# Delta rule: triangles laid in the partitions by block, matrix and head, and one store of the inverses per half of the rows in place of four

## The chip, the cores and the metric

The kernel runs on one core of one Trainium2 chip. The metric is the device time of one execution in microseconds (us). Times given as measured are the median of several runs; a profile is one further execution, recorded by the hardware profiler. A core has five engines that run their own instruction streams: TensorE (PE, with its weight loads PEld), VectorE (DVE), ScalarE (ACT), GpSimd (POOL) and SyncE (SP). DMA transfers are issued by SP (queue q1 in the profile), ACT (q10) and POOL (q0) and are moved by 16 DMA engines.

## The reference, cut to what matters

One layer of a bidirectional hybrid encoder on 256 tokens of width 2048. Branch B is a gated delta rule with 16 heads of width 128, forward and backward. The part that matters here is the unit lower triangular solve of each chunk:

```python
    a_mat = jnp.eye(CHUNK, dtype=jnp.float32) + (
        betac[..., :, None] * jnp.einsum('nbhid,nbhjd->nbhij', kc, kc) * decay_strict)
    t_mat = lax.linalg.triangular_solve(
        a_mat, jnp.broadcast_to(jnp.eye(CHUNK, dtype=jnp.float32), a_mat.shape),
        left_side=True, lower=True, unit_diagonal=True)
    u = jnp.einsum('nbhij,nbhje->nbhie', t_mat, betac[..., None] * vc)
    w = jnp.einsum('nbhij,nbhjd->nbhid', t_mat, (betac * jnp.exp(gc))[..., None] * kc)
```

Beside it stand a chunkwise mLSTM branch, the merge of the two branches and a SwiGLU feed-forward part, all with float32 weights that are read once.

## The kernel before

The bulk of the work is matrix products against weights of 1 MB pieces that SP loads. Each piece is split on the chip into a high part by ACT (wh, L157 and L182) and a low part by DVE (wl, L158 and L183), and PE multiplies with both (L161, L163 and L200 to L203). PE runs in its own order, so a wl that is late holds it up.

The delta rule is woven between these products. The kernel uses chunks of 128 tokens, so a head has four matrices: forward and backward for each of two chunks. Of each matrix only the four diagonal blocks of 32x32 are inverted by elimination; the larger blocks follow by small products.

- `gdn_phase1(h)` (L537) makes the four matrices of head h in the tile mi, partitions = row of the matrix. POOL writes the 16 triangles of the head to the DRAM tile inst_d (four DMAs, L604, one for each diagonal block) and reads them back so that each triangle lies in one partition of the tile uu (one DMA, L607). Four heads make a group (GRP = 4), so uu has 64 partitions of 32x32 numbers. Before the change the 16 triangles of a head lie in 16 neighbouring partitions.
- `gdn_invert(g)` (L619) inverts the 64 triangles of group g on DVE, 30 steps of two instructions (L635, L641). After the step i = 16 the rows 16 to 31 are done, after the last step the rows 0 to 15. `store(rows)` (L625) writes such a half to the DRAM tile inv_d: four POOL DMAs, one for each head, each of 16 partitions (L627). A run of DRAM that is written in one piece has 32 numbers, 128 B.
- `gdn_blocks(g)` (L650) reads inv_d into cg with the four diagonal blocks stacked in the partitions: four POOL DMAs (L654) that wait until both halves are stored. DVE transposes the 32x32 blocks (L656) and mixes them into R (L660, L661); ACT copies them into X (L669) and UL (L674).
- `gdn_phase2(g, p)` (L677) does the products for two heads of the group; its first PE instruction is p1 (L689), which needs R.

The order of instructions on an engine is set by a scheduler with a model of durations of its own, except for those inside `order(...)`, which keep the order of the program. Between `invert(g)` and the first use of cg the main program (L857 to L863) puts eight steps of weight products (`fill(8)`), so that PE, ACT and DVE have work while the inverses go to DRAM and back. Times in the text are from the start of the span. Group 0 passes this place at about 284 to 305 us, group 1 at 472 to 490, group 2 at 658 to 682 and group 3 at 857 to 876.

A weight product is named by its job: o0 and o1, mb1, ma2, a2 and b4, b8, b12 are such jobs, and wl_o1_0_2 is the low part of the second half of the first piece of job o1.

Of the kernel before, what the change touches and what calls it, by code (L numbers as in the profile page):

```python
# [9 lines left out]
F32 = mybir.dt.float32  # L10
# [11 lines left out]
NH_B, DK_B = 16, 128  # L22
# [3 lines left out]
GRP = 4  # L26
# [26 lines left out]
def hybrid_block(ctx: ExitStack, tc: tile.TileContext, xr, nfr, crow, pk_d, cst_d, ada2, ada4, win0, winb, wint, wba, wbb, wo, wgu, wd, out, dbg=None):  # L53
    nc = tc.nc
    V, S, G, PE = nc.vector, nc.scalar, nc.gpsimd, nc.tensor
# [29 lines left out]
    def order(ins, yes=True):  # L85

        return tc.keep_in_program_order(ins) if yes else ins
# [168 lines left out]
    mb_d = [tc.dram_tile([P, 2, 512], F32, name=f"mb_d{g}") for g in range(4)]  # L256
    ob_d = [tc.dram_tile([4, P, T], F32, name=f"ob_d{g}") for g in range(4)]
    inst_d = [tc.dram_tile([64, 32, 32], F32, name=f"inst_d{g}") for g in range(NH_B // GRP)]
    inv_d = [tc.dram_tile([32, 4, 16, 32], F32, name=f"inv_d{g}") for g in range(NH_B // GRP)]

    hh, hl = (bigA.tile([P, KB // 2, 2, 2, P], F32R, tag="b16", name=n) for n in ("hh", "hl"))

# [179 lines left out]
    with ExitStack() as s0:  # L442
        w0 = pool(s0, "w0")

        x = w0.tile([P, KB, T], F32, name="x")
        ss = w0.tile([P, 2], F32, name="ssx")
        rows = w0.tile([P, T], F32, name="rows")
# [87 lines left out]
    uus = {}  # L535

    def gdn_phase1(h):  # L537
# [61 lines left out]
        g, hl_ = divmod(h, GRP)  # L599
        if g not in uus:  # L600
            uus[g] = bk.tile([64, 32, 32], F32, tag="uu", bufs=1, name=f"uu{g}")
        inst = inst_d[g][16 * hl_ : 16 * hl_ + 16]
        for b in range(4):
            G.dma_start(  # L604
                inst[4 * b : 4 * b + 4].rearrange("x j i -> j x i"), mi[32 * b : 32 * b + 32, :, 32 * b : 32 * b + 32]
            )
        G.dma_start(uus[g][16 * hl_ : 16 * hl_ + 16], inst)  # L607

        cc = ccs[h % NB]
        for b in range(4):  # L610
# [8 lines left out]
    def gdn_invert(g):  # L619

        uu = uus.pop(g)
        tmp = bk.tile([64, 256], F32, tag="utmp", bufs=1, name=f"utmp{g}")
        inv = inv_d[g].rearrange("j b (x h) i -> h (b x) j i", h=GRP)

        def store(rows):  # L625
            for e in range(GRP):
                G.dma_start(inv[e, :, rows], uu[16 * e : 16 * e + 16, rows])  # L627

        yield
        order(V.memset(uu.rearrange("p j i -> p (j i)")[:, ::33], 1.0))  # L630
        size = 0
        for i in range(30, 0, -1):
            w = 31 - i
            t3 = tmp[:, 0 : i * w].rearrange("p (j c) -> p j c", j=i)
            order(V.tensor_tensor(  # L635
                t3,
                uu[:, 0:i, i : i + 1].broadcast_to([64, i, w]),
                uu[:, i : i + 1, i + 1 :].broadcast_to([64, i, w]),
                ALU.mult,
            ))  # L640
            order(V.tensor_tensor(uu[:, 0:i, i + 1 :], uu[:, 0:i, i + 1 :], t3, ALU.add))  # L641
            if i == 16:
                store(slice(16, 32))
            size += i * w + 125
            if size > 720:
                size = 0
                yield
        store(slice(0, 16))

    def gdn_blocks(g):  # L650

        cg = bk.tile([P, 2, 512], F32, tag="uu", bufs=1, name=f"cg{g}")
        for b in range(4):
            G.dma_start(cg[32 * b : 32 * b + 32, 0], inv_d[g][:, b].rearrange("j x i -> j (x i)"))  # L654
        yield
        order(V.transpose(cg[:, 1], cg[:, 0]))  # L656
        F_, Bt, Ft, B_ = (cg[:, i // 2, (i % 2) * 256 : (i % 2 + 1) * 256].rearrange("p (m c) -> p m c", m=8) for i in range(4))

        def mix(dst, a, ca, b, cb):
            order(V.tensor_scalar(dst, b, cb, None, ALU.mult))  # L660
            order(V.scalar_tensor_tensor(dst, a, ca, dst, ALU.mult, ALU.add))  # L661

        mix(R[:, 0], Ft, even, Bt, odd)
        mix(R[:, 1], B_, even, F_, odd)
        yield
        for i, ab in enumerate(((Ft, Bt), (B_, F_))):
            for b in range(4):
                r = slice(32 * b, 32 * b + 32)
                order(S.activation(X[r, i, :, b % 2], ab[b // 2][r], AF.Copy))  # L669
            yield  # L670
        for i, a in enumerate((F_, B_)):
            for b in range(4):
                r = slice(32 * b, 32 * b + 32)
                order(S.activation(UL[r, i, :, r], a[r], AF.Copy))  # L674
            yield
# [133 lines left out]
    def stream(h0):  # L809
# [21 lines left out]
        while True:  # L831
            fill(1)
            yield True

    heads1 = {h: gdn_phase1(h) for h in range(NH_B)}
    after = (0, 1, 2, 1, 2, 2, 2, 2, 4, 0)
    last = (0, 1, 2, 1, 2, 2, 1, 1, 3, 0)
# [12 lines left out]
    def invert(g):  # L850
        gen = gdn_invert(g)
        next(gen)
        fill(4)
        for _ in gen:
            fill(1)

    invert(0)  # L857
    for g in range(4):
        blocks = gdn_blocks(g)
        next(blocks)  # L860
        fill(8)
        next(blocks)
        fill(1)  # L863
        pairs = [gdn_phase2(g, p) for p in range(2)]
        every[0] = (0, 2, 2, 2)[g]
        for p in range(2):
            pieces = stream(4 * g + 2 * p + 4)
            for n in range(1, 10):
                next(pairs[p], None)
                if p == 0:  # L870
                    next(blocks, None)
                for _ in range(after[n] if g < 3 else last[n]):
                    next(pieces)
            for _ in pairs[p]:
                pass

            if g < 3:
                while 4 * g + 2 * p + 5 not in heads:
                    next(pieces)
        if g < 3:  # L880
            fills.insert(0, z_job(g + 1))
            every[0] = 0
            invert(g + 1)
# [327 lines left out]
    for j in range(FB // 4):  # L1211
# [4 lines left out]
        for e2 in range(2):  # L1216
            px = gps(f"pxf{j}_{e2}")
            for e in range(2):
                f = 2 * e2 + e
                for t in range(2):  # L1220
                    PE.transpose(px[:, e * T + t * P : e * T + (t + 1) * P], sg[:, t, f * P : (f + 1) * P], ident)
            b = 4 * j + 2 * e2
# [143 lines left out]
```

## Time and profile before

| | us |
|---|---|
| median of 3 runs | 2038.97 (2037.25 to 2042.45) |
| the profiled execution | 2036.88 |
| its span, first to last instruction | 2035.0 |
| PE busy | 1956.7 (96%) |
| DVE busy | 1394.1 (69%) |
| ACT busy | 1050.0 (52%) |
| POOL busy | 106.4 (5%) |

In the timeline a row has the start in us, the duration in us, the engine, the line, the operation, what it writes and reads, how often (x) in a row, and in brackets the idle time of the engine before it and what ended that. The rows of a stretch of time give the length, then for each engine the busy time, then the TensorE clock that was granted (1.00 is full speed), the share of the time in which the DMA engines moved data, and GB/s. The rows of DMA queues give packets, MB and the share of the 16 engines' time. An engine is counted as waiting only if it had nothing else that it was allowed to do.

### The profile page before, as it was taken

The numbers are of one execution on the slowest core, as the hardware profiler recorded it, in microseconds if no ns is written. First come the engines' busy times: TensorE is split into PE (matmuls) and PEld (weight loads), VectorE is DVE, ScalarE is ACT, GpSimd is POOL, SyncE is SP. The second block draws the span as 40 slices with busy tenths as digits, with TensorE's granted clock in tenths as the row PEclk, the third lists the DMA queues.
The fourth block names the chain that finished last, engine by engine and source line by source line (L and its number), as shares of the span: only waits on it lengthen the run. The fifth ranks groups of instructions, "written<-read, shape, count | busy, mean of one in ns | idle before, by whom it ended". The sixth has DMA issues, their size and how long they took to land.

```text
span 2035.0 us, 27065 instructions
## 1 busy us (share of the span) xinstructions
PE 1956.7 (96%) x10374; PEld 1706.4 (84%) x10374; DVE 1394.1 (69%) x2059; ACT 1050.0 (52%) x1582; POOL 106.4 (5%) x205
## 2 busy tenths in 40 slices
PE   8999999999999899999899999999999999999997
PEld 6777879988888788988878788778888888888886
DVE  5778777777889588855677679866666665555554
ACT  3147547755775577565444444554444444444443
POOL 0002210010101010100200000000000000000000
PEclk9999999999999899999999999999999999999999
DMA  9986664556766465766987669656767666566563
GB/s 399 420 325 222 178 215 153 190 171 220 241 230 197 178 211 212 243 238 240 360 297 264 212 245 390 256 186 249 252 244 262 235 246 212 204 206 204 199 200 142
DMA packets 78962, 485.64 MB, mean 239 GB/s; under 512 B 10585, under 2 KB 15969, under 8 KB 24433
## 3 DMA queue, kind: packets, MB, share of 16 engines
q1 hardware_dynamic: 63360, 450.95, 61.2%
q0 software_dynamic: 8160, 17.88, 3.8%
q10 hardware_dynamic: 7314, 15.10, 2.0%
q8 instruction: 81, 1.33, 0.3%
q14 instruction: 47, 0.39, 0.1%
HBM read 467.07 MB, written 16.82 MB: 238 GB/s over the span
## 4 chain that ended last, share of the span: by engine, by line
PE 70%; DMA 11%; DVE 9%; ACT 6%; issue 2%; POOL 1%; ACTq 0%; SPq 0%; DVEq 0%; POOLq 0%
PE acc_up L200 4%; PE acc_up L203 4%; PE acc_up L201 4%; PE acc_d L201 4%; PE acc_d L200 4%; PE acc_d L203 4%; PE acc_gt L201 4%; PE acc_gt L200 4%; PE acc_gt L203 4%; PE acc_b L161 3%; DMA ra<-ada 3%; DMA ada<-ada 2%; PE acc_o L203 2%; PE acc_o L200 2%; PE acc_o L201 2%
## 5 line engine op out<-in xcount | busy, mean ns | idle before, releaser
L183 DVE TENSOR_TENSOR wl_d<-raw_d,wh_d 128x1024 fp32r<-128x1024 f32 x88 | 107.5, 1225 | 105.4 <-ACT wh_d L182 103.1
L183 DVE TENSOR_TENSOR wl_up<-raw_up,wh_up 128x1024 fp32r<-128x1024 f32 x88 | 107.6, 1225 | 100.4 <-ACT wh_up L182 100.4
L126 DVE SCALAR_TENSOR_TENSOR ada<-ada,crow 128x2048 f32<-128x2048 f32 x64 | 146.6, 2290 | 24.1 <-DMA ada<-ada 24.0
L182 ACT ACTIVATE wh_d<-raw_d 128x1024 fp32r<-128x1024 f32 x88 | 92.9, 1056 | 124.5 <-PE acc_d L201 114.3
L183 DVE TENSOR_TENSOR wl_gt<-raw_gt,wh_gt 128x1024 fp32r<-128x1024 f32 x88 | 107.7, 1224 | 69.9 <-ACT wh_gt L182 68.4
L182 ACT ACTIVATE wh_up<-raw_up 128x1024 fp32r<-128x1024 f32 x88 | 92.9, 1057 | 120.9 <-PE acc_up L201 71.6
L161 PE MATMUL acc_b<-hh,wh_b 128*128 128x256 f32 x576 | 142.0, 288 | 9.6 <-ACT wh_b L157 8.0
L182 ACT ACTIVATE wh_gt<-raw_gt 128x1024 fp32r<-128x1024 f32 x88 | 92.9, 1055 | 108.9 <-PE acc_gt L201 61.3
L161 PE MATMUL acc_b<-hl,wh_b 128*128 128x256 f32 x576 | 139.6, 284 | 0.0
L201 PE MATMUL acc_gt<-wh_gt,hfl 128*128 128x512 f32 x352 | 136.9, 389 | 0.0
L200 PE MATMUL acc_gt<-wh_gt,hfh 128*128 128x512 f32 x352 | 135.6, 385 | 0.0
L200 PE MATMUL acc_up<-wh_up,hfh 128*128 128x512 f32 x352 | 133.4, 379 | 0.0
L201 PE MATMUL acc_up<-wh_up,hfl 128*128 128x512 f32 x352 | 133.4, 379 | 0.0
L200 PE MATMUL acc_d<-wh_d,ffh 128*128 128x512 f32 x344 | 130.8, 380 | 0.0
L201 PE MATMUL acc_d<-wh_d,ffl 128*128 128x512 f32 x344 | 130.5, 379 | 0.0
L161 PEld LDWEIGHTS acc_b<-hh,wh_b 128*128 128x128 f32 x576 | 114.6, 199 | 10.2 <-ACT wh_b L157 8.5
L511 PE MATMUL first<-x,raw 128*128 128x256 f32 x512 | 114.5, 382 | 6.6 <-ACT x L504 6.6
L511 PEld LDWEIGHTS first<-x,raw 128*128 128x128 f32 x512 | 96.0, 190 | 25.1 <-ACT x L504 12.6
L161 PEld LDWEIGHTS acc_b<-hl,wh_b 128*128 128x128 f32 x576 | 114.8, 199 | 0.0
L300 DVE SCALAR_TENSOR_TENSOR cv<-pad,pk,cv 128x256 f32<-128x256 f32 x192 | 90.8, 481 | 20.2 <-ACT cv L298 18.2
L158 DVE TENSOR_TENSOR wl_b<-raw_b,wh_b 128x1024 fp32r<-128x1024 f32 x72 | 86.9, 1220 | 23.7 <-ACT wh_b L157 20.6
L182 ACT ACTIVATE wh_o<-raw_o 128x1024 fp32r<-128x1024 f32 x64 | 67.4, 1056 | 60.1 <-PE acc_o L201 27.2
(369 smaller groups left out, 5016.4 us busy)
## 6 DMA issues: line engine op xcount, KB each, us to landing
ada<-ada SPq DMA_DIRECT2D x64, 1024.0 KB, 5.2
raw_gt<-wgu SPq DMA_DIRECT2D x44, 1024.0 KB, 5.0
raw_up<-wgu SPq DMA_DIRECT2D x44, 1024.0 KB, 4.9
raw_d<-wd SPq DMA_DIRECT2D x44, 1024.0 KB, 4.9
raw_b<-winb SPq DMA_DIRECT2D x36, 1024.0 KB, 5.1
ra<-ada SPq DMA_DIRECT2D x32, 1025.0 KB, 15.7
raw<-win SPq DMA_DIRECT2D x16, 1024.0 KB, 14.5
raw_z<-wint SPq DMA_DIRECT2D x16, 1024.0 KB, 5.1
```

Source lines behind the costliest of these rows:

```text
L126: V.scalar_tensor_tensor(raw, raw, 1.0, row_c[:, :D], ALU.mult, ALU.mult, accum_out=mod[:, c0 + b : c0 + b + 1])
L158: V.tensor_tensor(wl, raw[:, k0 : k0 + 8], wh.bitcast(F32), ALU.subtract)
L161: PE.matmul(o, wh[:, k], both(x, k0 + k).rearrange("p a b -> p b a"), start=k0 + k + i == 0, stop=False)
L182: order(S.activation(wh, raws[u][:, k0 : k0 + 2], AF.Copy), early)
L183: order(V.tensor_tensor(wl, raws[u][:, k0 : k0 + 2], wh.bitcast(F32), ALU.subtract), early)
L200: order(PE.matmul(ps[t], tok(xh, kk, t), turns(wh[:, k]), start=kk == 0, stop=False), early and steps > 1)
L201: PE.matmul(ps[t], tok(xl, kk, t), turns(wh[:, k]), start=False, stop=False)
L203: PE.matmul(ps[t], tok(xh, kk, t), turns(wl[:, k]), start=False, stop=kk == last)
L300: V.scalar_tensor_tensor(cv, pd[:, i : i + T], w[i], cv, ALU.mult, ALU.add)
L511: PE.matmul(first[o], raw[:, o], x[:, b], start=b == 0 and o % 2 == 0, stop=b == KB - 1 and o % 2 == 1)
```

## The change

The partition of a triangle in uu is no longer 16 x head + 4 x block + matrix but 16 x block + 4 x matrix + head (head within the group). The load of a head's triangles therefore goes to every fourth partition. The partitions of uu then lie in the order in which inv_d holds the triangles, so that `store(rows)` is one DMA of 64 partitions in place of four of 16. The bytes of inv_d, the four loads of cg and all computation are as they were.

```diff
-    inv_d = [tc.dram_tile([32, 4, 16, 32], F32, name=f"inv_d{g}") for g in range(NH_B // GRP)]
+    inv_d = [tc.dram_tile([32, 64, 32], F32, name=f"inv_d{g}") for g in range(NH_B // GRP)]
...
-        G.dma_start(uus[g][16 * hl_ : 16 * hl_ + 16], inst)
+        G.dma_start(uus[g][hl_::GRP], inst)
...
-        inv = inv_d[g].rearrange("j b (x h) i -> h (b x) j i", h=GRP)
...
         def store(rows):
-            for e in range(GRP):
-                G.dma_start(inv[e, :, rows], uu[16 * e : 16 * e + 16, rows])
+            G.dma_start(inv_d[g][rows].rearrange("j p i -> p j i"), uu[:, rows])
...
-            G.dma_start(cg[32 * b : 32 * b + 32, 0], inv_d[g][:, b].rearrange("j x i -> j (x i)"))
+            G.dma_start(cg[32 * b : 32 * b + 32, 0], inv_d[g][:, 16 * b : 16 * b + 16].rearrange("j m i -> j (m i)"))
```

The scheduler also moves instructions of the weight products around the place where cg is waited for. The order of PE stays as it was. On DVE, group 1, before the change (cg1 is the tile of the inverses, R and wl as above):

```order
L183 TENSOR_TENSOR wl_o1_0_0_4026<-raw_o1_0_4023,wh_o1_0_0_4025 128x1024
L183 TENSOR_TENSOR wl_o1_0_2_4047<-raw_o1_0_4023,wh_o1_0_2_4046 128x1024
L656 STREAM_TRANSPOSE cg1_3894<-cg1_3894 128x512
L660 TENSOR_SCALAR R_1108<-cg1_3894,cst_75 128x256
L158 TENSOR_TENSOR wl_b8_0_0_4077<-raw_b8_0_4074,wh_b8_0_0_4076 128x1024
L661 SCALAR_TENSOR_TENSOR R_1108<-cg1_3894,cst_75,R_1108 128x256
L660 TENSOR_SCALAR R_1108<-cg1_3894,cst_75 128x256
L661 SCALAR_TENSOR_TENSOR R_1108<-cg1_3894,cst_75,R_1108 128x256
```

The same place on DVE after the change:

```order
L183 TENSOR_TENSOR wl_o1_0_0_4014<-raw_o1_0_4011,wh_o1_0_0_4013 128x1024
L654 STREAM_TRANSPOSE cg1_3882<-cg1_3882 128x512
L658 TENSOR_SCALAR R_1108<-cg1_3882,cst_75 128x256
L659 SCALAR_TENSOR_TENSOR R_1108<-cg1_3882,cst_75,R_1108 128x256
L658 TENSOR_SCALAR R_1108<-cg1_3882,cst_75 128x256
L183 TENSOR_TENSOR wl_o1_0_2_4035<-raw_o1_0_4011,wh_o1_0_2_4034 128x1024
L659 SCALAR_TENSOR_TENSOR R_1108<-cg1_3882,cst_75,R_1108 128x256
L158 TENSOR_TENSOR wl_b8_0_0_4065<-raw_b8_0_4062,wh_b8_0_0_4064 128x1024
```

The last wl that PE needs ahead of p1, wl_o1_0_2, stood ahead of the transposition of cg1 and now stands three instructions behind it; wl_b8_0_0 moves two places back. On DVE, group 3, before the change:

```order
L158 TENSOR_TENSOR wl_a2_3_0_8067<-raw_a2_3_8064,wh_a2_3_0_8066 128x1024
L158 TENSOR_TENSOR wl_a2_3_8_8100<-raw_a2_3_8064,wh_a2_3_8_8099 128x1024
L656 STREAM_TRANSPOSE cg3_7852<-cg3_7852 128x512
L660 TENSOR_SCALAR R_1108<-cg3_7852,cst_75 128x256
L661 SCALAR_TENSOR_TENSOR R_1108<-cg3_7852,cst_75,R_1108 128x256
L660 TENSOR_SCALAR R_1108<-cg3_7852,cst_75 128x256
L183 TENSOR_TENSOR wl_ma2_0_0_8146<-raw_ma2_0_8143,wh_ma2_0_0_8145 128x1024
L661 SCALAR_TENSOR_TENSOR R_1108<-cg3_7852,cst_75,R_1108 128x256
```

The same place on DVE after the change:

```order
L158 TENSOR_TENSOR wl_a2_3_0_8043<-raw_a2_3_8040,wh_a2_3_0_8042 128x1024
L654 STREAM_TRANSPOSE cg3_7828<-cg3_7828 128x512
L658 TENSOR_SCALAR R_1108<-cg3_7828,cst_75 128x256
L659 SCALAR_TENSOR_TENSOR R_1108<-cg3_7828,cst_75,R_1108 128x256
L658 TENSOR_SCALAR R_1108<-cg3_7828,cst_75 128x256
L659 SCALAR_TENSOR_TENSOR R_1108<-cg3_7828,cst_75,R_1108 128x256
L158 TENSOR_TENSOR wl_a2_3_8_8076<-raw_a2_3_8040,wh_a2_3_8_8075 128x1024
L183 TENSOR_TENSOR wl_ma2_0_0_8122<-raw_ma2_0_8119,wh_ma2_0_0_8121 128x1024
```

Here wl_a2_3_8, the last low part that PE needs ahead of p1, moves from ahead of the transposition to behind the second R. In group 0 wl_o0_2_0, which stood behind the first instruction on R, stands behind the third; group 2 keeps its order.

On ACT, group 1, the order before (X is what ACT copies from cg1, ev_mb1 empties a PSUM buffer that PE wants again for job b8):

```order
L182 ACTIVATE wh_o1_0_2_4046<-raw_o1_0_4023 128x1024
L157 ACTIVATE wh_b8_0_0_4076<-raw_b8_0_4074 128x1024
L313 ACTIVATE ev_mb1_4017<-acc_mb1_0_3870 128x512
L313 ACTIVATE ev_mb1_4017<-acc_mb1_1_3871 128x512
L669 ACTIVATE X_1109<-cg1_3894 32x8x32
L314 DMA mb_d1_111<-ev_mb1_4017 128x1024
```

The same place on ACT after the change:

```order
L182 ACTIVATE wh_o1_0_2_4034<-raw_o1_0_4011 128x1024
L667 ACTIVATE X_1109<-cg1_3882 32x8x32 x4
L157 ACTIVATE wh_b8_0_0_4064<-raw_b8_0_4062 128x1024
L313 ACTIVATE ev_mb1_4005<-acc_mb1_0_3861 128x512
L313 ACTIVATE ev_mb1_4005<-acc_mb1_1_3862 128x512
L314 DMA mb_d1_111<-ev_mb1_4005 128x1024
```

The four copies into X now stand ahead of wh_b8_0_0 and of ev_mb1.

## Prediction

> **What bounds the kernel now.** I read the page first: the span and the busy shares.
>
> ```profile
> span 2035.0 us, 27065 instructions
> PE 1956.7 (96%) x10374; PEld 1706.4 (84%) x10374; DVE 1394.1 (69%) x2059; ACT 1050.0 (52%) x1582; POOL 106.4 (5%) x205
> ```
>
> PE is nearly always busy, so this change can only pay through the few places where PE stops. Next I asked who waits for the stores (the view of the tile inv_d) and what size they have (the list of DMA issues).
>
> ```profile
> L627 POOL DMA_DIRECT2D inv_d<-uu x32: 562/562/593, 266.5 to 858.3; - x32
>   DVE cg L656: 28.4, 4
>   POOL cg L654: 22.0, 4
> inv_d<-uu POOLq DMA_DIRECT2D x32, 32.0 KB, 3.4
> ```
>
> POOL takes 562 ns to issue one store of 32 KB. It waits 22.0 us in four groups for the stores before it may issue the loads of cg, and DVE waits 28.4 us for these loads. Whether PE pays is seen in the timeline. Group 0:
>
> ```profile
> 284.24 2.23 POOL L627 DMA_DIRECT2D inv_d<-uu  x4 [15.45 <-DVE uu L641]
> 291.24 1.99 POOL L654 DMA_DIRECT2D cg<-inv_d  x4 [4.77 <-DMA inv_d<-uu]
> 299.95 0.71 DVE L656 STREAM_TRANSPOSE cg<-cg 128x512 f32<-128x512 f32 x1 [8.62 <-DMA cg<-inv_d]
> 300.81 1.22 DVE L183 TENSOR_TENSOR wl_o<-raw_o,wh_o 128x1024 fp32r<-128x1024 f32 x1
> 302.08 1.54 PE L203 MATMUL acc_o<-wl_o,hh 128*128 128x512 f32 x4 [3.50 <-DVE wl_o L183]
> ```
>
> So store, wait, load, wait, transposition, wl lie in one chain, and PE stands 3.50 us at its end, until 302.08. The eight steps of filling are too short by that. The stretches around the stops add a second price, the granted clock (the number before the last two):
>
> ```profile
> 298.50:302.00 3.50, 0.08 (x1) 0.00 (x0) 2.05 (x4) 1.21 (x3) 0.00 (x0) 1.00 0.02 6
> 302.00:309.00 7.00, 6.92 (x31) 6.68 (x32) 5.27 (x8) 3.62 (x6) 0.00 (x0) 0.55 0.28 81
> 485.60:488.20 2.60, 0.05 (x1) 0.00 (x0) 2.51 (x5) 1.69 (x5) 0.00 (x0) 1.00 0.37 150
> 678.50:682.00 3.50, 3.44 (x18) 3.44 (x19) 2.36 (x4) 0.49 (x2) 0.00 (x0) 0.56 0.63 192
> ```
>
> After the stop of 3.50 us PE runs 7.0 us at 0.55, which loses 7.0 x 0.45 = 3.15 us; after group 2's stops it loses 3.5 x 0.44 = 1.5 us. After the stop of group 1 (the third row) the clock stayed at 1.00.
>
> Groups 1, 2 and 3, from the timeline:
>
> ```profile
> 472.18 2.22 POOL L627 DMA_DIRECT2D inv_d<-uu  x4 [16.47 <-DVE uu L641]
> 479.04 1.99 POOL L654 DMA_DIRECT2D cg<-inv_d  x4 [4.64 <-DMA inv_d<-uu]
> 484.62 1.03 PE L203 MATMUL acc_o<-wl_o,hh 128*128 128x512 f32 x4
> 485.69 0.71 DVE L656 STREAM_TRANSPOSE cg<-cg 128x512 f32<-128x512 f32 x1 [6.32 <-DMA cg<-inv_d]
> 488.22 1.08 PE L689 MATMUL p<-R,cc 128*128 128x32 f32 x8 [2.57 <-DVE R L661]
> ```
>
> ```profile
> 657.87 2.22 POOL L627 DMA_DIRECT2D inv_d<-uu  x4 [13.10 <-DVE uu L641]
> 665.33 1.99 POOL L654 DMA_DIRECT2D cg<-inv_d  x4 [5.23 <-DMA inv_d<-uu]
> 672.11 0.71 DVE L656 STREAM_TRANSPOSE cg<-cg 128x512 f32<-128x512 f32 x1 [6.48 <-DMA cg<-inv_d]
> 675.03 1.13 PE L203 MATMUL acc_mb<-wl_mb,hh 128*128 128x512 f32 x4 [1.40 <-DVE wl_mb L183]
> 678.56 0.58 PE L161 MATMUL acc_b<-hh,wh_b 128*128 128x256 f32 x1 [1.59 <-ACT ev_ma L313]
> ```
>
> ```profile
> 856.63 2.22 POOL L627 DMA_DIRECT2D inv_d<-uu  x4 [16.49 <-DVE uu L641]
> 866.20 2.00 POOL L654 DMA_DIRECT2D cg<-inv_d  x4 [7.35 <-DMA inv_d<-uu]
> 870.72 1.06 PE L163 MATMUL acc_a<-hh,wl_a 128*128 128x256 f32 x8
> 872.18 0.71 DVE L656 STREAM_TRANSPOSE cg<-cg 128x512 f32<-128x512 f32 x1 [6.99 <-DMA cg<-inv_d]
> 873.79 1.05 PE L689 MATMUL p<-R,cc 128*128 128x32 f32 x8 [2.02 <-DVE R L661]
> ```
>
> All that hangs on these transfers is 3.50 + 2.57 + 1.40 + 1.59 + 2.02 = 11.1 us of stops and 4.7 us of slow clock, 15.8 us together. More than that the change cannot give.
>
> **What the store costs now, and will cost.** The four stores of group 0 were issued from 284.24 to 286.47. The DMA queues of the stretches 284.2 to 287.0 (first row), 287.7 to 289.4 (second) and 289.4 to 290.2 (third) tell when they ran:
>
> ```profile
> q0 software_dynamic: 49, 0.07, 18.1%
> ...
> q1 hardware_dynamic: 87, 0.71, 98.9%
> ...
> q0 software_dynamic: 64, 0.07, 23.2%
> ```
>
> Two stores (2 x 32 KB = 0.07 MB) ran before 287.0. Then a weight load on q1 held the engines at 98.9%, and in this stretch the answer has no row for q0 at all. The other two stores, though issued by 286.47, ran after 289.4, and POOL went on at 291.24. Groups 1 and 2 show the same 6.86 and 7.46 us from the first issue to the loads (479.04 - 472.18, 665.33 - 657.87), group 3 9.57 us. The Trainium skill ("DMA: Bandwidth & Descriptors", Queues, rings and completion order) says that each engine takes turns between its queue rows packet by packet; the trace does not bear that out here, since no packet of q0 moved for 1.7 us.
>
> *One issue in place of four* saves three of 562 ns, 1.7 us, if the issue of 64 partitions costs the same. It writes four times as many pieces of 128 B as one old store. From below: 0.56 us. From above: four times that, 2.25 us, no saving. The widest POOL issue in the trace has 128 x 4 pieces of 1 KB:
>
> ```profile
> 968.31 1.57 POOL L895 DMA_DIRECT2D o<-ob_d  x2 [100.11 <-ACT wh_a L157]
> ```
>
> 0.79 us each for twice the pieces of an old store. I take 0.8 us, so 1.4 us saved.
>
> *One place in the queue in place of four* is the larger part. All packets of the one store stand in the queue from its issue on, so they should run where the first two stores ran, ahead of the weight load. The second old store's last completions fell before 287.7 and POOL needed 291.24 - 290.2 = 1.0 us after the last packets of the others, so the loads of cg would be issued at about 288.7, 2.5 us earlier. They meet the same bursts of weights, so DVE's start moves by more or by less. Call the shift of DVE's transposition S. Bounds: 0 (the store finishes no earlier than four do) and about 5 us (store and load each escape one burst of some 2.5 us). I take S = 3, near the 2.5.
>
> **The sum.** The order of DVE changed, and that must be set against S. The pitch of its instructions after a transposition, from group 3:
>
> ```profile
> 873.56 0.35 DVE L660 TENSOR_SCALAR R<-cg,cst 128x256 f32<-128x256 f32 x1
> 873.82 1.22 DVE L183 TENSOR_TENSOR wl_ma<-raw_ma,wh_ma 128x1024 fp32r<-128x1024 f32 x1
> 874.96 0.48 DVE L661 SCALAR_TENSOR_TENSOR R<-cg,cst,R 128x256 f32<-128x256 f32 x1
> ```
>
> A wl behind three instructions on R starts 873.82 - 872.18 = 1.64 us after the transposition starts and ends 2.86 us after; behind four of them, some 0.4 us later, 3.25.
>
> - Group 0: PE went on 302.08 - 299.95 = 2.13 us after the transposition; now 2.86, 0.73 later. With S = 3 PE gains 2.27 of its 3.50; a stop of 1.2 us should keep the clock (2.57 did), 3.15 more. Sum 5.4.
> - Group 1: wl_o1_0_2 now ends at 485.69 - S + 2.86, its four matmuls take 0.9, so p1 starts at 489.45 - S against 488.22. With S = 3: 1.8 us gained. The four copies into X ahead of ev_mb1 on ACT are hidden as long as p1 is later than they are.
> - Group 2: order unchanged, both stops are shorter than S; the second hangs on ACT, whose copies into X start with the transposition. 1.40 + 1.59 + 1.5 = 4.5.
> - Group 3: wl_a2_3_8 ends at 872.18 - S + 3.25, eight matmuls take 0.9 to 1.06, so p1 starts at about 876.4 - S against 873.79. With S = 3: 0.4.
>
> Sum 12.1 us. What is late next is DVE itself: it gains only S where PE gains the clock too, so if later products hang on DVE, groups 0 and 2 carry 3 us each and the sum is 8.2. I take 10 us between them.
>
> The rest costs nothing. The load into every fourth partition has the same 16 rows; DVE waited 3.4 us in all for this load, which bounds it in both directions:
>
> ```profile
>   DMA uu<-inst_d: 3.4, 1
> ```
>
> The first half's store has over 15 us until the second (POOL idles 15.45 us between them in group 0), and behind the second on POOL stand only the loads of cg that need it.
>
> The profiled execution took 2036.88 us, 2.1 us under the median of the runs, 2038.97. So 2036.9 - 10 = 2026.9 by the profile, 2029.0 as a median. A measurement of this kernel tells about 0.3% from no change, 6.1 us: below 2032.9 is faster, above 2045.1 slower.
>
> **The rivals.**
>
> *A, the forecast* (chance 0.53): S between 2 and 5, gain 5 to 16 us, 2023 to 2034.
>
> *B, only the issues are saved* (0.32): the bursts catch the store or the loads of cg as before, S = 1.7 or less. Group 0 gains 1.0 and perhaps the clock's 3.15, group 1 0.5, group 2 1.7 to 4.5, group 3 loses 0.9: 2.3 to 8.2 us, in the middle 5, 2034. For it: the loads of cg are not changed, and they too wait behind q1. Against it: two of four old stores always escaped. By the rule that the Trainium skill states on "DMA: Bandwidth & Descriptors", turns packet by packet, no store would wait behind a burst, and 2034 is what it would give.
>
> *C, slower* (0.15): the one store ends when the four did, because making its descriptors takes 2.25 us and its tail comes behind the burst. Then S = 0 and the new DVE order bites: group 0 loses 0.7, group 1 1.2, group 3 2.6. The stops become 3.9 us in group 1 (484.62 to 488.55) and 4.7 us in group 3 (870.72 to 875.43), longer than the 3.50 that cost the clock, some 3 us each. Loss 4.5 to 10.5, 2043 to 2049. It decides at S below 1.2 in group 1 and below 2.6 in group 3. For it: the number of 128 B pieces does not fall. Against it: the trace has 562 ns for 256 pieces and 0.79 us for 512, which is no proportion. The Trainium skill ("DMA: Bandwidth & Descriptors", SWDGE vs HWDGE vs iDMA) speaks for it in so far as it says that a DMA of GpSimd has its descriptors computed by software; a cost in proportion to their number is case C.
>
> **How the numbers follow.** The likeliest case gives 2029.0. The range 2022 to 2041 reaches from A's best, 2023, with 1 us for the scatter of the runs (2037.25 to 2042.45 before), over B to no gain at all, 2039, with 2 us for that scatter; it leaves out C. Faster: nine tenths of A and a seventh of B, 0.52. Slower: three quarters of C, 0.11. The same: the rest, 0.37.
>
> **What would show it.** Right: POOL issues one store in 0.6 to 1.0 us; the loads of cg follow 4 to 5 us after the store's issue in place of 6.9 to 9.6; DVE's wait for cg falls from 28.4 to some 16 us; after group 0 PE's clock stays at 1.00. Wrong: a store issue above 2 us; the loads still 7 us after the store; or S as forecast and PE stopped elsewhere, so that the time stays.

## The result, and the profile after

| | before | after |
|---|---|---|
| median, us | 2038.11 (2034.85 to 2045.39, 8 runs) | 2028.69 (2022.85 to 2033.69, 8 runs) |
| the profiled execution | 2036.88 | 2033.09 |
| its span | 2035.0 | 2031.3 |

The ratio is 0.9951, with a 95% interval from 0.9931 to 0.9972: faster by 9.4 us, or 0.5%. The forecast was 2029.0. The profiled execution of the changed kernel took 4.4 us more than its median and shows 3.7 us of gain in the span. Its rows are therefore read place by place, and the medians decide on the total.

The page after the change, the busy shares:

```profile
PE 1960.8 (97%) x10374; PEld 1710.8 (84%) x10374; DVE 1393.5 (69%) x2059; ACT 1049.3 (52%) x1582; POOL 95.6 (5%) x181
```

PE's idle time, span less busy time, fell from 2035.0 - 1956.7 = 78.3 to 2031.3 - 1960.8 = 70.5 us. Its busy time rose by 4.1 us for the same 10374 matmuls, at a mean granted clock of 0.984 against 0.987. The difference is the 3.7 us.

The view of the tile inv_d after the change answers the first question, what a store costs and who waits:

```profile
L625 POOL DMA_DIRECT2D inv_d<-uu x8: 824/838/868, 265.7 to 849.7; - x8
  DVE cg L654: 20.9, 4
  POOL cg L652: 14.4, 4
```

One store of 64 partitions is issued in 838 ns, in place of four times 562. POOL's wait for the stores fell from 22.0 to 14.4 us, DVE's wait for cg from 28.4 to 20.9.

The timeline after the change, groups 0 and 2, store, loads and transposition (lines stand two lower than before):

```profile
283.45 0.83 POOL L625 DMA_DIRECT2D inv_d<-uu  x1 [16.85 <-DVE uu L639]
287.42 2.01 POOL L652 DMA_DIRECT2D cg<-inv_d  x4 [3.14 <-DMA inv_d<-uu]
294.96 0.71 DVE L654 STREAM_TRANSPOSE cg<-cg 128x512 f32<-128x512 f32 x1 [4.42 <-DMA cg<-inv_d]
...
654.35 0.83 POOL L625 DMA_DIRECT2D inv_d<-uu  x1 [14.81 <-DVE uu L639]
658.61 2.01 POOL L652 DMA_DIRECT2D cg<-inv_d  x4 [3.43 <-DMA inv_d<-uu]
664.57 0.71 DVE L654 STREAM_TRANSPOSE cg<-cg 128x512 f32<-128x512 f32 x1 [2.81 <-DMA cg<-inv_d]
```

The loads of cg follow the store by 3.97 and 4.26 us, where it was 7.00 and 7.46. From the store to the transposition it takes 11.51 and 10.22 us, where it was 15.71 and 14.24. PE does not stop in these two places any more: in the stretches 297.70 to 301.10 and 671.30 to 678.00 it is busy for 3.32 of 3.40 and 6.48 of 6.70 us, at full clock.

```profile
297.70:301.10 3.40, 3.32 (x26) 3.12 (x26) 3.03 (x5) 2.76 (x3) 0.00 (x0) 1.00 0.01 2
671.30:678.00 6.70, 6.48 (x58) 6.29 (x57) 2.34 (x5) 0.61 (x2) 0.00 (x0) 1.00 0.87 323
```

Group 1 after the change is another picture. POOL, DVE, SP (its queue, SPq) and PE in order of time:

```profile
466.29 0.82 POOL L625 DMA_DIRECT2D inv_d<-uu  x1 [17.86 <-DVE uu L639]
470.41 2.00 POOL L652 DMA_DIRECT2D cg<-inv_d  x4 [3.30 <-DMA inv_d<-uu]
476.97 0.71 DVE L654 STREAM_TRANSPOSE cg<-cg 128x512 f32<-128x512 f32 x1 [5.72 <-DMA cg<-inv_d]
478.62 1.22 DVE L183 TENSOR_TENSOR wl_o<-raw_o,wh_o 128x1024 fp32r<-128x1024 f32 x1
479.87 0.33 SPq L125 DMA_DIRECT2D ada<-ada  x1
479.89 1.13 PE L203 MATMUL acc_o<-wl_o,hh 128*128 128x512 f32 x4 [1.00 <-DVE wl_o L183]
485.11 2.29 DVE L126 SCALAR_TENSOR_TENSOR ada<-ada,crow 128x2048 f32<-128x2048 f32 x1 [3.33 <-DMA ada<-ada]
487.32 0.69 DVE L688 TENSOR_TENSOR pt<-p,cst 128x512 f32<-128x512 f32 x1
488.07 1.20 PE L696 MATMUL p<-R,pt 128*128 128x32 f32 x8 [3.47 <-DVE pt L688]
```

The store and the loads are quick here too (4.12 us), and the stop of 2.57 us ahead of p1 is gone. But wl_o1_0_2 now runs behind the transposition. PE waits 1.00 us for it. It also ends only at 478.62 + 1.22 = 479.84, and at 479.87 SP issues the load of the next 1 MB of the ada weights, which goes into the same three raw buffers (both have the tag raw). The load lands at 485.11. DVE has reached its instruction on ada 3.33 us earlier and stands there, with pt, the input of p2, queued behind it. So PE stops 3.47 us ahead of p2 (L696), where it had not stopped before. The same two rows before the change, the ada load and p2:

```profile
479.39 0.33 SPq L125 DMA_DIRECT2D ada<-ada  x1
...
491.89 1.00 PE L698 MATMUL p<-R,pt 128*128 128x32 f32 x8
```

A row of PE without brackets had no wait. There wl_o1_0_2 ran from 478.14 to 479.36, and the ada load was issued 0.03 us later, as it is after the change. But the transposition came only at 485.69, 6.3 us behind that load; now it comes 2.9 us ahead of it.

Group 3 after the change:

```profile
849.66 0.82 POOL L625 DMA_DIRECT2D inv_d<-uu  x1 [18.01 <-DVE uu L639]
855.07 2.01 POOL L652 DMA_DIRECT2D cg<-inv_d  x4 [4.58 <-DMA inv_d<-uu]
863.41 0.71 DVE L654 STREAM_TRANSPOSE cg<-cg 128x512 f32<-128x512 f32 x1 [7.98 <-DMA cg<-inv_d]
866.85 1.28 PE L163 MATMUL acc_a<-hh,wl_a 128*128 128x256 f32 x8 [3.05 <-DVE wl_a L158]
...
874.67 0.97 PE L696 MATMUL p<-R,pt 128*128 128x32 f32 x8
```

Here wl_a2_3_8 (L158) waits behind the transposition and the four instructions on R, and PE stops 3.05 us for it, more than the 2.02 it had lost to R before. Behind both new stops the clock falls. The stretches in which the stop lies and those that follow, after the change:

```profile
485.46:488.88 3.42, 0.81 (x8) 0.82 (x8) 3.42 (x4) 0.00 (x0) 0.00 (x0) 1.00 0.20 37
488.88:492.29 3.41, 3.41 (x18) 3.41 (x18) 2.76 (x4) 0.59 (x3) 0.00 (x0) 0.50 0.97 324
...
864.34:867.76 3.42, 0.91 (x8) 0.91 (x9) 3.35 (x6) 0.88 (x1) 0.00 (x0) 1.00 0.00 0
867.76:871.17 3.41, 3.41 (x15) 3.14 (x14) 3.04 (x4) 2.22 (x6) 0.00 (x0) 0.50 0.97 325
871.17:874.59 3.42, 3.42 (x9) 2.69 (x9) 0.00 (x0) 1.06 (x1) 0.00 (x0) 0.50 0.79 320
```

3.41 us at half clock in group 1 and 6.83 us in group 3 lose 1.7 and 3.4 us. Between these two executions group 1 lost 1.00 + 3.47 - 2.57 + 1.7 = 3.6 us. About 1.1 us of this came back some 20 us later, at a stop for another low part that was 1.65 us before (at 509.49) and is 0.59 us now. Group 3 is counted from the store to p2, since p2 waited before. The same row before the change:

```profile
878.36 1.08 PE L698 MATMUL p<-R,pt 128*128 128x32 f32 x8 [0.85 <-DVE pt L690]
```

From the store to p2 it took 878.36 - 856.63 = 21.73 us before and 874.67 - 849.66 = 25.01 after, so group 3 lost 3.3 us.

The theory from here: the merged store brings the loads of cg forward in all four groups, by its one place in the queue, and the new order of DVE takes a part back in groups 1 and 3. The rivals: the gain is the saved issue time alone, or comes from the layout; the losses in groups 1 and 3 come from DMA bandwidth or from the clock and not from the two low parts.

### The profile page after: what moved, and what is told of

Its sections match the earlier page's. It is cut to its first block, busy times and chain, and to the rows that moved or that the text cites. A ratio compares the mean times of both kernels' runs of the same rounds, so it can differ in the third digit from the quotient of the medians.

```text
span 2031.3 us, 27030 instructions
## 1 busy us (share of the span) xinstructions
PE 1960.8 (97%) x10374; PEld 1710.8 (84%) x10374; DVE 1393.5 (69%) x2059; ACT 1049.3 (52%) x1582; POOL 95.6 (5%) x181
## 4 chain that ended last, share of the span: by engine, by line
PE 52%; DMA 2%; DVE 2%; ACT 1%; issue 1%; POOL 0%; ACTq 0%; POOLq 0%; DVEq 0%
PE acc_up L201 4%; PE acc_up L203 4%; PE acc_up L200 4%; PE acc_d L201 4%; PE acc_d L200 4%; PE acc_d L203 4%; PE acc_gt L201 4%; PE acc_gt L200 4%; PE acc_gt L203 3%; PE acc_o L203 1%; PE acc_o L200 1%; PE acc_o L201 1%; PE acc_yb L203 1%; PE acc_ya L203 1%; PE acc_yb L201 1%; PE acc_yb L200 1%
## 5 line engine op out<-in xcount | busy, mean ns | idle before, releaser
L161 PEld LDWEIGHTS acc_b<-hh,wh_b 128*128 128x128 f32 x576 | 115.0, 200 | 10.2 <-ACT wh_b L157 10.2
L158 DVE TENSOR_TENSOR wl_b<-raw_b,wh_b 128x1024 fp32r<-128x1024 f32 x72 | 86.9, 1219 | 23.1 <-ACT wh_b L157 22.5
```

What stands on the lines that cost most here:

```text
L158: V.tensor_tensor(wl, raw[:, k0 : k0 + 8], wh.bitcast(F32), ALU.subtract)
L161: PE.matmul(o, wh[:, k], both(x, k0 + k).rearrange("p a b -> p b a"), start=k0 + k + i == 0, stop=False)
```

## The experiments

Ratios are to the kernel before, run beside each experiment on the same chip, with a 95% interval.

**The layout alone.** The new partitions, but four stores for a half; every engine keeps the order of before.

```diff
-            G.dma_start(inv_d[g][rows].rearrange("j p i -> p j i"), uu[:, rows])
+            for e in range(4):
+                G.dma_start(inv_d[g][rows, 16 * e : 16 * e + 16].rearrange("j p i -> p j i"), uu[16 * e : 16 * e + 16, rows])
```

> The new layout of the partitions, but each half stored by four DMAs of 16 partitions again; the order of every engine is that of the kernel before. Theory (the gain comes from one issue and one place in the queue, not from the layout): ratio to before 1.000, within 0.997 to 1.003; each store issue 0.56 us; the loads of cg follow 6.9 to 9.6 us after the first store's issue, and the transposition of group 0 starts near 300. Rival (the layout itself pays, by the load of uu or by the bytes that a store writes): ratio 0.995 as the changed kernel has.

Measured: 2036.83 us, ratio 1.0003 (0.9989 to 1.0017). The loads of cg follow the first of four store issues by 7.26, 6.82, 7.17 and 9.62 us, as before. The layout by itself pays nothing that shows; it only makes one store possible.

**The second half alone.** Rows 16 to 31 go in four stores, rows 0 to 15 in one; the order is that of the changed kernel.

```diff
-            G.dma_start(inv_d[g][rows].rearrange("j p i -> p j i"), uu[:, rows])
+            n = 4 if rows.start else 1
+            q = 64 // n
+            for e in range(n):
+                G.dma_start(inv_d[g][rows, q * e : q * e + q].rearrange("j p i -> p j i"), uu[q * e : q * e + q, rows])
```

> Only the store of rows 0 to 15, the last one ahead of the loads of cg, is one DMA; rows 16 to 31 go in four. The order of PE, DVE, ACT and SP is that of the changed kernel. Theory (the first half has over 15 us to spare): the whole gain, ratio to before 0.995, and loads of cg 4.0 to 5.4 us after the store. Rival (the first half's packets also count, as they share the queue): half of the gain, 0.9975.

Measured: 2028.55 us, ratio 0.9954 (0.9938 to 0.9970). The whole gain is there, so merging the first half's stores pays nothing that shows: they have over 15 us to spare. The loads of cg follow the store by 3.93, 4.07, 4.58 and 6.41 us, the last of them later than expected.

This run has the changed kernel's order on PE, DVE, ACT and SP, so it is a second execution of the same places. Group 1 again stops ahead of p2, by 3.58 us. Group 3 stops only 1.48 us for wl_a2_3_8 and keeps its clock. The transposition comes 12.64 us after the store there, in place of 13.75.

**Last in the queue.** Three stores of the old size, into a spare DRAM tile, are issued just ahead of the merged one. They add 96 KB of writes that nobody reads. All engines but POOL have the order of the kernel before, so the run is compared with that kernel, and no loss by the new order is in it.

```diff
         def store(rows):
+            for e in range(3 if rows.start == 0 else 0):
+                order(G.dma_start(spare[e].rearrange("j p i -> p j i"), uu[0:16, rows]))
-            G.dma_start(inv_d[g][rows].rearrange("j p i -> p j i"), uu[:, rows])
+            order(G.dma_start(inv_d[g][rows].rearrange("j p i -> p j i"), uu[:, rows]))
```

> The changed kernel with three further stores of the old size (16 partitions of uu, 32 KB each, into a spare DRAM tile) issued just ahead of the second half's store, so that its packets come last in the queue; the order of DVE and ACT around cg is that of the kernel before. Theory of the place in the queue: the store's data comes behind the burst of weights, the loads of cg follow the first of the four issues by 7 us or more, 5.5 us or more after the last one's, ratio 0.999 to 1.003. Rival (only issue time counts): the loads follow 1.7 + 4.0 to 4.3 = 5.7 to 6.0 us after the first issue in groups 0 to 2, ratio 0.997.

Measured: 2038.85 us, ratio 1.0012 (0.9998 to 1.0027): the gain is gone. Group 0 on POOL, then the DMA queues from 287.0 to 289.0 (two rows) and q0 from 289.0 to 290.3:

```profile
284.21 1.68 POOL L627 DMA_DIRECT2D spare<-uu  x3 [16.85 <-DVE uu L642]
285.88 0.83 POOL L628 DMA_DIRECT2D inv_d<-uu  x1
292.00 1.99 POOL L655 DMA_DIRECT2D cg<-inv_d  x4 [5.29 <-issue]
```

```profile
q1 hardware_dynamic: 87, 0.71, 88.4%
q0 software_dynamic: 12, 0.00, 0.3%
...
q0 software_dynamic: 71, 0.16, 34.7%
```

The loads follow 7.79 us after the first issue, and 6.12 us after the merged store's own, where the same store took 3.97 in the changed kernel. Issued 1.67 us later, it waits behind the burst on q1 (0.00 MB of q0 from 287.0 to 289.0) and moves only then. By issue time alone the loads would have come at 285.88 + 3.97 = 289.85, not at 292.00. The place in the queue is worth about these 2.15 us (0.03 of the 0.16 MB that ran from 289.0 to 290.3 belong to the third spare store), more than the 4 x 0.56 - 0.84 = 1.4 us of saved issues.

For comparison, the changed kernel's store from 284.5 to 285.6, ahead of the burst:

```profile
q0 software_dynamic: 36, 0.13, 62.7%
```

All of its 0.13 MB (64 partitions x 16 x 128 B) ran in this stretch.

**The two low parts kept ahead.** In groups 1 and 3 the ninth step of filling is put ahead of the transposition in the program, and the low parts of these nine steps keep the program's order. By that wl_o1_0_2 and wl_a2_3_8 come ahead of the transposition.

```diff
-            order(V.tensor_tensor(wl, raws[u][:, k0 : k0 + 2], wh.bitcast(F32), ALU.subtract), early)
+            order(V.tensor_tensor(wl, raws[u][:, k0 : k0 + 2], wh.bitcast(F32), ALU.subtract), early or kept[0])
...
-            V.tensor_tensor(wl, raw[:, k0 : k0 + 8], wh.bitcast(F32), ALU.subtract)
+            order(V.tensor_tensor(wl, raw[:, k0 : k0 + 8], wh.bitcast(F32), ALU.subtract), kept[0])
...
-        fill(8)
+        kept[0] = g in (1, 3)
+        fill(9 if kept[0] else 8)
+        kept[0] = False
         next(blocks)
-        fill(1)
+        fill(0 if g in (1, 3) else 1)
```

> The changed kernel, with the two low parts wl_o1_0_2 (group 1) and wl_a2_3_8 (group 3) kept ahead of the transposition of cg on DVE; nothing else moves but copies into X on ACT in group 1. Theory (their new place behind the transposition costs PE 1.0 us ahead of p1, delays the release of the raw buffer, so that the next ada load starts at 479.9 and p2 stands 3.5 us, and costs 3.1 us in group 3, with 1.7 and 3.4 us of slow clock behind these two): the stop ahead of p2 in group 1 is under 0.5 us, the ada load is issued 4 us or more before the transposition ends, the stop in group 3 is under 1 us; up to 12 us faster than the changed kernel's profile, ratio to before 0.990 to 0.992. Rival (the ada load is late because DMA bandwidth is short there, and the clock is lost somewhere else anyway): the stop ahead of p2 stays at 3 us or more, ratio 0.994 to 0.996.

Measured: 2019.06 us (2012.07 to 2023.52), ratio 0.9911 (0.9888 to 0.9934), the fastest kernel of this study. The profiled execution took 2012.07 us, the fastest of the six and 7 us under their median. Its rows, the page's shares, the ada load on SP, the transposition and p2 of group 1, and the stretch of group 3 in which the stop was:

```profile
span 2010.3 us, 27030 instructions
PE 1946.2 (97%) x10374; PEld 1698.8 (85%) x10374; DVE 1393.6 (69%) x2059; ACT 1049.5 (52%) x1582; POOL 95.3 (5%) x181
```

```profile
472.01 0.33 SPq L127 DMA_DIRECT2D ada<-ada  x1
...
474.81 0.71 DVE L656 STREAM_TRANSPOSE cg<-cg 128x512 f32<-128x512 f32 x1 [2.83 <-DMA cg<-inv_d]
...
481.67 0.98 PE L698 MATMUL p<-R,pt 128*128 128x32 f32 x8
```

```profile
847.50:855.00 7.50, 7.50 (x62) 7.31 (x62) 5.05 (x8) 4.06 (x8) 0.00 (x0) 1.00 0.56 186
```

PE does not stop ahead of p2, nor ahead of p1 at 478.10. The ada load is issued 2.8 us ahead of the transposition, not 2.9 us behind it (4 us were expected). Group 3 has no stop, with PE busy for 7.50 of 7.50 us at full clock.

**Each low part alone.** As above with `g == 1`, and with `g == 3`.

> As the kernel with both low parts kept ahead, but in group 1 alone (wl_o1_0_2 ahead of the transposition). Theory (each of the two places costs for itself: group 1 has 1.0 + 3.5 us of stops and 1.7 us of slow clock, group 3 has 3.1 and 3.4): about half of the 9.6 us that both together gave, ratio to before 0.992 to 0.9935; the ada load is issued at about 472, p2 doesn't wait, and group 3 still stops 2.5 to 3.5 us ahead of the last matmuls with wl_a. Rival (a stop that is removed in group 1 only lets PE arrive earlier in group 3 and wait longer there): group 3 stops by 5 us or more, ratio 0.9945 to 0.996.

Measured: 2022.08 us, ratio 0.9921 (0.9903 to 0.9938).

> The same in group 3 alone (wl_a2_3_8 ahead of the transposition). Theory: the other half, ratio to before 0.992 to 0.9935; the stop in group 3 is under 1 us, and group 1 still has its stops of 1 us ahead of p1 and 3 to 3.5 us ahead of p2. Rival (group 3 costs nothing, the clock would be slow there in any case): ratio 0.995.

Measured: 2025.46 us, ratio 0.9936 (0.9918 to 0.9955). The stop that stays in each, group 3 of the first and group 1 of the second:

```profile
859.89 2.08 PE L165 MATMUL acc_a<-hh,wl_a 128*128 128x256 f32 x8 [2.50 <-DVE wl_a L160]
```

```profile
487.90 1.19 PE L698 MATMUL p<-R,pt 128*128 128x32 f32 x8 [3.99 <-DVE pt L690]
```

In the first, the ada load is issued at 472.95 and PE doesn't wait for p2. In the second, group 3 has no stop. Its ratio lies at the edge of what was expected, and the stop of 3.99 us ahead of p2 is longer than the 3 to 3.5 expected.

Against the changed kernel's 0.9951 the place in group 1 is worth 0.0030 (6 us) and that in group 3 0.0015 (3 us), together 0.0045, and both at once gave 0.0040. Within the noise they add up. The intervals of the two overlap with each other and with the changed kernel's, so the split is less sure than the sum, and the 3 us of group 3 are not clear of no difference. The rival that PE only waits longer later falls: group 3 still stops 2.50 us, not 5.

**pt ahead of ada.** On DVE pt of group 1 is kept ahead of the first ada instruction; wl_o1_0_2 stays behind the transposition.

```diff
-            V.scalar_tensor_tensor(raw, raw, 1.0, row_c[:, :D], ALU.mult, ALU.mult, accum_out=mod[:, c0 + b : c0 + b + 1])
+            order(V.scalar_tensor_tensor(raw, raw, 1.0, row_c[:, :D], ALU.mult, ALU.mult, accum_out=mod[:, c0 + b : c0 + b + 1]), part == 2 and b == 0)
...
-        V.tensor_tensor(
+        order(V.tensor_tensor(
             pt0.rearrange("p m (b c) -> p m b c", b=4),
...
-        )
+        ), (g, p) == (1, 0))
```

> The changed kernel with wl_o1_0_2 left behind the transposition, but on DVE the product pt of group 1 kept ahead of the first ada instruction. The scheduler then orders some instructions behind group 1 in another way, so only the trace of group 1 is read. Theory (p2 waits because pt stands in DVE's queue behind an ada instruction whose load is issued only when wl_o1_0_2 has released its raw buffer): the ada load is still issued within 0.1 us of the end of wl_o1_0_2, but p2 waits less than 1 us. Rival (pt itself or p1 is late): p2 still waits about 3 us.

Measured (one run, 2026.24 us), group 1 of its timeline:

```profile
481.23 1.22 DVE L183 TENSOR_TENSOR wl_o<-raw_o,wh_o 128x1024 fp32r<-128x1024 f32 x1
482.48 0.33 SPq L125 DMA_DIRECT2D ada<-ada  x1
485.59 2.36 DVE L158 TENSOR_TENSOR wl_b<-raw_b,wh_b 128x1024 fp32r<-128x1024 f32 x2 [1.21 <-ACT wh_b L157]
488.61 1.08 PE L696 MATMUL p<-R,pt 128*128 128x32 f32 x8 [1.40 <-DVE pt L688]
```

The ada load is issued at 482.48, 0.03 us after wl_o1_0_2 ends (481.23 + 1.22 = 482.45): the raw buffer sets it. The stop ahead of p2 falls from 3.47 to 1.40 us, not below 1 as expected, since in this order two wl_b of 2.36 us stand ahead of pt. The larger part of the stop was ada in DVE's queue.

## Why the prediction was right, and where it was not

*The store.* The issue was taken as 0.8 us and measured 0.84. The number of 128 B pieces grew fourfold and the time by 838 / 562 = 1.5, so case C's first condition, a cost in proportion, did not hold.

*The place in the queue.* The loads of cg were to follow 4 to 5 us after the store; they follow after 3.97, 4.12, 4.26 and 5.41 us. Case B, the issues alone, fell with the run that put three stores ahead.

*The shift S.* From the store's issue to the transposition it took 15.71, 13.51, 14.24 and 15.55 us before, and 11.51, 10.68, 10.22 and 13.75 after. S is 4.20, 2.83, 4.02 and 1.80, on average 3.2; 3 was taken. In the run with the second half alone, with the same order, it is 4.28, 3.64, 4.19 and 2.91, on average 3.8. So S scatters by group and by execution, and 3 is a choice that came out near its middle.

*Group 0* was to give 5.4 us and gave about 6.6 (6.3 matmul by matmul): its stop of 3.50 is gone, not reduced to 1.2, since S is 4.20 there, and the clock's 3.15 came back as forecast. *Group 2* was to give 4.5 us, and both its stops and the slow clock behind them are gone: matmul by matmul, the gain from 655 to 686 us of the kernel before is 4.9 us.

*Group 1* is the step that failed. The working ended at p1 and had p1 start at 489.45 - S, 1.8 us gained. For p1 that holds: with PE and the store some 5.9 us earlier than before (466.29 against 472.18) and S = 2.83 it gives 480.7, and p1 started at 480.86, behind the four matmuls of 479.89. What was not followed is the raw buffer that wl_o1_0_2 releases. Its next user is the ada load, and behind ada on DVE stands pt, which p2 needs. The prediction's sentence that the rest costs nothing overlooked that chain. In place of a gain of 1.8 us the profiled execution lost 3.6, and keeping wl_o1_0_2 ahead gave 6 us in the medians. The 3.6 us are the difference of two single executions. The one before had paid no clock in group 1, while the run with the layout alone, which has the same order, stopped there for 3.21 us and then ran two stretches, 6.83 us, at half clock.

*Group 3* was put at a gain of 0.4 us, with the warning in case C that below S = 2.6 the new order costs more than the store gives, and the clock as well. S was 1.80, and the group lost 3.3 us in the profiled execution. In the run with the second half alone, with the same order, S was 2.91, and the group gained 1.6 us. So case C was right as a mechanism for one group in one execution and wrong for the sum.

*DVE's wait for cg* was to fall to some 16 us and fell to 20.9. DVE now waits in the time in which it used to make wl_o1_0_2 and wl_a2_3_8, 1.2 us each; with both kept ahead the wait is 12.6 us. The rest is not explained by the two low parts: with the second half alone, in the same order, the wait is 17.4 us.

*The sum.* The forecast of 10 us met 9.4, but by other terms than the ones written down, and in part by luck. PE has the same order in all these runs, so the gain of each place can be read matmul by matmul against the kernel before, from ahead of the place to some 10 to 30 us behind it. For the changed kernel the four groups give 6.3 - 2.1 + 4.9 - 3.3 = 5.8 us in its profiled execution, and 6.3 - 1.4 + 4.9 + 1.6 = 11.4 us in the run with the second half alone (3.7 and 9.0 us over the whole span). Groups 0 and 2 are steady, groups 1 and 3 are not, and the 10 was itself a choice between 12.1 and 8.2.

With the order kept the same store is worth 2036.64 - 2019.06 = 17.6 us in the medians, so the new order takes some 8 us of it back in groups 1 and 3 (0.9951 - 0.9911 of 2037; by the two intervals, an estimate, anything from 2 to 14 us). The 17.6 is above the 15.8 us called the most that the change can give. The interval of the ratio (13.4 to 22.8 us) holds 15.8, so the excess is not sure. But the bound left out a wait that hangs on the transfers too, the 0.85 us ahead of p2 in group 3. In the profiled execution with the order kept the four groups give 6.1 + 3.5 + 4.9 + 3.0 = 17.5 us.

That execution was 24.7 us shorter than the one before: PE's idle time is 2010.3 - 1946.2 = 64.1 us, 14.2 less, and its busy time 10.5 us less. Of the stretches of 3.41 us in which the clock goes (see below), 14 ran at half clock before, 17 after the change and 8 with the order kept. Six fewer, at 1.7 us each, are 10.2 us, nearly all of the busy time. Three of the six are those behind the stops of groups 0 and 2; why three fewer occur elsewhere was not tried.

## What to carry to other kernels

A small transfer that shares DMA engines with large loads is worth issuing in one piece ahead of the burst; here the time saved at issue was the smaller part. When a scheduler answers an edit by moving an instruction, follow not only who needs its result but also which buffer it releases, which load waits for that buffer, and what is queued behind that load's consumer. Low parts that PE needs soon should not stand behind an instruction that waits for DRAM: with two of them pinned ahead, the same edit gave about twice the gain.

## What was not expected of the hardware

**The clock goes by fixed stretches of 3.41 us.** The stretches of the prediction were cut by eye. Cut every 3.413 us from one change of the clock, all further changes of the clock in the same trace fall on a cut, to within 0.02 us, in each of the nine traces. Before the change, groups 0 and 1:

```profile
299.26:302.67 3.41, 0.59 (x3) 0.53 (x4) 2.72 (x5) 1.83 (x5) 0.00 (x0) 1.00 0.00 0
302.67:306.08 3.41, 3.41 (x16) 3.23 (x15) 3.00 (x5) 2.78 (x3) 0.00 (x0) 0.50 0.00 0
...
483.58:486.99 3.41, 2.07 (x10) 1.48 (x8) 1.30 (x3) 0.55 (x2) 0.00 (x0) 1.00 0.19 65
486.99:490.40 3.41, 2.18 (x19) 2.18 (x20) 3.38 (x5) 3.12 (x5) 0.00 (x0) 1.00 0.39 156
490.40:493.80 3.40, 3.40 (x32) 3.40 (x32) 3.40 (x5) 1.06 (x1) 0.00 (x0) 1.00 0.45 120
```

The stop of 3.50 us put 2.82 us of idle time into one stretch (3.41 - 0.59), and the next two, 6.83 us, ran at half clock. The stop of 2.57 us fell on a cut, 1.34 and 1.23 us, and cost no clock. The prediction read from this stop that 2.57 us keep the clock; it was the cut that kept it. After the change 2.61 us of idle time fell into one stretch (485.46 to 488.88), and the clock was lost. Over the nine traces, from 250 us on, each of the 75 full-clock stretches with 1.9 us or more of idle PE was followed by one at half clock; of the 107 with 0.8 to 1.9 us 13 were. The Trainium skill ("TensorE: Matmul & The Clock Gate", Part 1) gives a free-running window of 3413 ns, and the trace agrees. It calls one idle window the condition for half clock; here windows that were 76 to 83% idle were enough (2.61 of 3.42, 2.82 of 3.41), and the measurement decides. The price of a stop thus depends on where in the window it falls. That is probably one reason why executions of one kernel differ: those of the changed kernel had mean clocks from 0.982 to 0.988.

**A queue that stands still beside a burst.** From 286.5 to 291.0 after the change, with the loads of cg issued from 287.42 on, q1 had the engines and one packet of q0 is recorded:

```profile
q1 hardware_dynamic: 237, 1.81, 102.2%
q0 software_dynamic: 1, 0.00, 0.0%
```

The store had escaped the burst, and the loads behind it met the next one: of the 7.54 us from their issue to the transposition (287.42 to 294.96) 3.6 passed with none of their data moved. That they meet the same bursts of weights was forecast. DVE was idle from 287.70 to 289.32, and none of the data moved in that time either, so the wait is not for a DVE instruction. Whether the engines serve q1 first, or the loads' packets come to them late while q1 is busy, is not told apart here.
